# Centring the output projection's weights and the residual ahead of the layer norm of a hybrid decoder step

## The chip, the cores and the metric

One core of one Trainium2 chip. The metric is the device time of one execution in microseconds, the median of the runs shown; lower is better.

## The reference

One layer of a decoder over 1024 prompt tokens and 8 sample tokens (N = 1032 columns), d = 2048. The input projection feeds four head groups: A (gated DeltaNet), B (RWKV-7), C (forgetting attention, with a paged cache of 4096 positions for the samples) and D (causal pooling). Their gated outputs go through one output projection, and the result is normalised:

```python
gated = jnp.concatenate([o_A * _silu(z_A), o_B * _silu(z_B), o_C * _silu(z_C), o_D * _silu(z_D)], axis=-1)
out = jnp.einsum('nte,ed->ntd', gated, P['w_out'])
y = _layernorm(ALPHA_DN * x + out, P['ln_g'], P['ln_b'])
# _layernorm: mu = mean(x); var = mean((x - mu)^2); (x - mu) * rsqrt(var + 1e-5) * g + b
```

## The kernel before

Everything is held transposed, channels on partitions and tokens in columns. A float32 product is made of three fp32r matmuls (`mm3`, L306): weights and data are each split into a rounded half (`whi`, a cast on ACT, L302) and the rest (`wlo`, a subtraction on DVE, L303). Matmuls run on PE.

**Input projection.** 57 tiles of 128 output channels, each sixteen contraction tiles by three column groups of 344. Beside it run *fillers*: generators that `fill` (L316) advances four times a tile, each by its rate in yields per fill; what they issue between two yields stands at that place in program order. A scheduler then lays the instructions of each engine in one fixed order by its own estimate of their times, earlier program order first, so that an engine that is free runs ahead. Tiles 17 to 32 (`inputs`) are group A's; beside them run the preparation of A's operands (rate 1.6) and `start_b` (rate 1): the triangular inverses of B (`invert`, two pairs of heads) and the recurrent step of B for the samples (`sample_b`). In the 24 tiles that follow (`inputs_cd`, 96 fills) the inverses of A and the decode over the cached keys run at rate 1.6, the chains of B and A, the branch D and the first of branch C at rate 1. In `invert` the diagonal blocks go through a DRAM scratch (`UT`) and back into the tile `ivB` (L1176), one yield later 16 small matmuls read it (L1182), then a second set of small transfers fills `ivB` (L1190), and after one more yield the second set of matmuls follows (L1195). SP issues these transfers; it also issues the decay rows (`aogb`, `aobb`) and the stores of A's preparation.

**Attention** of branch C follows (`mixing`, about 1720 to 1920 us), with the decode over cached values (`decode_v`) as a filler that runs on into the third output pass.

**Output projection.** The contraction runs in four passes, one for each head group (`order`), because the groups are ready at different times. `self.y` (sixteen tiles of 128 x 1032) is the accumulator in SBUF. `out_pass` (L1700) does passes 0 to 2: for each tile `ct` 36 matmuls into three PSUM banks of tag `o` (five in all), then y += ps on DVE (L1720). In pass 2 it adds the residual first: y += ALPHA * x (L1714), x loaded on SP. Weights come as blocks of 128 x 512, fetched by `fetch` on ACT's queue into two `raw` buffers, split into two buffers each, and in the last pass into tiles that stay (`wkh`, `wkl`).

`out_last` (L1723) does pass 3 in three column groups of 392, 384 and 256, so that the normalisation of one group runs beside the matmuls of the next. PSUM starts with a matmul of a constant matrix of -16/2048 with the rounded y[0] (`mneg`, `yr`, L1765), which takes off a rough mean. Each tile is added to y (L1769), y is summed over tiles on DVE (L1775) and its square on ACT (L1776) and GpSimd, in the last group DVE (L1777). Then `norm` sums both over partitions with two matmuls (L1741), copies them (L1742), forms the variance, and per tile subtracts the mean (L1750), multiplies by the inverse root (L1751), both split between DVE and GpSimd by `NPOOL`, applies gain and bias on ACT (L1752) and stores on SP (L1753). `norm` is a filler of rate 1: its steps for a group stand between the tiles of the next.

Of the kernel before, what the change touches and what calls it, by code (L numbers as in the profile page):

```python
# [11 lines left out]
ALU = mybir.AluOpType  # L12
# [167 lines left out]
class Kernel:  # L180
# [94 lines left out]
    def weights(self, pool, srcs, pieces, keep=1 << 30):  # L275


        self.wp, self.wsrc, self.wraw, self.wsplit, self.wkeep, self.wn = pool, srcs, {}, {}, keep, pieces
# [855 lines left out]
    def invert(self, pool, br, pair, BD):  # L1134
# [42 lines left out]
        yield True  # L1177
# [13 lines left out]
        yield True  # L1191
# [494 lines left out]

    def gated(self, br, gp, stage):

        nc = self.nc
        gh = self.t(gp, [128, 4, N], "gh", F32R)  # L1690
        gl = self.t(gp, [128, 4, N], "gl", F32R)
        for i in range(4):
            r = self.t(stage, [128, N], "ostg")
            nc.sync.dma_start(r, self.G[4 * br + i])
            nc.scalar.copy(gh[:, i], r)  # L1695
            nc.vector.tensor_tensor(gl[:, i], r, gh[:, i].bitcast(F32), op=ALU.subtract)
        return gh, gl

    def out_pass(self, i, g, stage):
# [3 lines left out]
        for ct in range(16):  # L1703
# [19 lines left out]
    def out_last(self, i, g, stage, pool):  # L1723


# [10 lines left out]
        def norm(s, n, st):  # L1736
            s1, s2 = st
            sq = self.t(pool, [128, GROUPS[0]], "sq", bufs=2)[:, :n]
# [17 lines left out]
        for n in GROUPS:  # L1756
            s = slice(g0, g0 + n)
            st = [self.t(pool, [128, GROUPS[0]], x, bufs=2)[:, :n] for x in ("s1", "s2")]
            for ct in range(16):
# [5 lines left out]
                nc.tensor.matmul(ps, lhsT=mneg, rhs=yr[:, s], start=True, stop=False)  # L1765
                for j in range(4):
                    self.mm3(ps, hi[:, j], lo[:, j], gh[:, j, s], gl[:, j, s], False, j == 3)
                y = self.y[ct][:, s]
                nc.vector.tensor_tensor(y, y, ps, op=ALU.add)  # L1769
                if ct == 0:  # L1770
                    nc.vector.tensor_copy(st[0], y)
                    nc.scalar.activation(st[1], y, AF.Square)
                else:
                    sq = self.t(pool, [128, GROUPS[0]], "sq", bufs=2)[:, :n]
                    nc.vector.tensor_tensor(st[0], st[0], y, op=ALU.add)  # L1775
                    nc.scalar.activation(sq, y, AF.Square)  # L1776
                    (nc.gpsimd if ct <= SPOOL[GROUPS.index(n)] else nc.vector).tensor_tensor(st[1], st[1], sq, op=ALU.add)  # L1777
                self.fill()
            self.add(norm(s, n, st), 1)
# [4 lines left out]
    def build(self):  # L1784
# [10 lines left out]
        self.UT = tc.dram_tile([4, 16, 32, 32], F32, name="ut")  # L1795
        self.lfd = tc.dram_tile([8, 32, 1024], F32, name="lfd")
# [9 lines left out]
        with P(name="const", bufs=1) as cp, P(name="psum", bufs=2, space=PSUM) as self.psum0:  # L1806
# [18 lines left out]
            with P(name="psum2", bufs=2, space=PSUM) as self.psum1:  # L1825
                R = dict(side="right")
                with P(name="wo", bufs=2, **R) as wp, P(name="ost", bufs=2, **R) as sp, P(name="y", bufs=1, **R) as yp, \
# [3 lines left out]
                    self.weights(wp, [self.I["wo"][ct][:, 4 * br:4 * br + 4] for br in order for ct in range(16)], 1, 48)  # L1831
                    with P(name="g1", bufs=1) as g1:
# [13 lines left out]
                        self.out_pass(2, g[2], sp)  # L1846
                        self.drain()
# [6 lines left out]
    def inputs(self, cp, sp):  # L1854
# [19 lines left out]
        with P(name="aprep", bufs=1, **R) as ap:  # L1874
# [3 lines left out]
            self.add(self.start_b(), 1)  # L1878
# [14 lines left out]
    def start_b(self):  # L1893

        yield from self.inverses("B")
        with self.tc.tile_pool(reuse_waits="tile", name="smpB", bufs=1) as pool:
            yield from self.sample_b(pool)

# [68 lines left out]
```

## Time and profile before

| | us |
|---|---|
| runs shown | 2399.39, 2399.89 (median), 2400.68 |
| the profiled execution, its own time | 2396.94 |
| its span, first to last instruction | 2395.2 |
| busy: PE / PEld / DVE / ACT / GpSimd | 2282.6 / 2023.0 / 1364.7 / 938.4 / 295.0 |
| mean granted TensorE clock | 0.979 of full speed |

Matmuls are pipelined: the time from the start of one to the start of the next is what one costs, not its listed duration. PE is the matmul row, PEld its weight load, DVE is VectorE, ACT ScalarE, POOL GpSimd, SP the queue of SyncE. Idle time of an engine that is not the bottleneck costs nothing.

### The profile page before, as it was taken

The page shows a single profiled execution, that of the slowest core. Times are in us where ns is not written, and L with a number is a line of the kernel's source. Part 1 is how long each engine was busy: PE and PEld are TensorE (multiplying, and loading weights), DVE is VectorE, ACT ScalarE, POOL GpSimd, SP SyncE. Part 2 cuts the span into 40 slices and gives each one's busy share as a digit, 9 for nine tenths or more (in the row PEclk, how much of TensorE's full clock was granted, in tenths as well). Part 3 has the DMA queues.
Part 4 walks back from the last instruction along what each step waited for, and adds up shares of the span by engine and source line. Part 5 has one row for each costly group of instructions (what it writes and reads, how often), then busy time and mean ns, then how long its engine had stood idle before and what let it go on. Part 6 is the DMA issues. An engine that isn't in the chain of part 4 may idle for free. (4 is left out here: it accounts for less than half of the span.)

```text
span 2395.2 us, 47251 instructions
## 1 busy us (share of the span) xinstructions
PE 2282.6 (95%) x17640; PEld 2023.0 (84%) x17640; DVE 1364.7 (57%) x2676; ACT 938.4 (39%) x1853; POOL 295.0 (12%) x408
## 2 busy tenths in 40 slices
PE   8999999999899999999999999999899999999984
PEld 8999999998899999787787877899755578889984
DVE  4665757677576557432222245555578644564598
ACT  5644445434454444121111122454366665211244
POOL 0000000000000000103111121100132110100175
PEclk9999999999999999999999999999999999999997
DMA  6133323545523336778878888653488775683212
GB/s 215 56 100 95 104 85 95 151 106 120 113 81 94 89 107 142 172 187 264 274 250 283 259 273 288 232 161 107 124 260 248 223 282 192 219 304 129 88 63 88
DMA packets 369664, 402.44 MB, mean 168 GB/s; under 512 B 204877, under 2 KB 228350, under 8 KB 368666
## 3 DMA queue, kind: packets, MB, share of 16 engines
q1 hardware_dynamic: 307698, 263.83, 37.3%
q10 hardware_dynamic: 50056, 101.60, 13.9%
q0 software_dynamic: 11680, 33.99, 4.3%
q8 instruction: 139, 2.28, 0.4%
q14 instruction: 91, 0.75, 0.1%
HBM read 314.56 MB, written 84.67 MB: 167 GB/s over the span
## 5 line engine op out<-in xcount | busy, mean ns | idle before, releaser
L308 PE MATMUL pj<-xh,wlo 128*128 128x344 f32 x2688 | 873.1, 326 | 16.7 <-DVE wlo L303 8.6
L309 PE MATMUL pj<-xl,whi 128*128 128x344 f32 x2688 | 871.5, 324 | 0.0
L310 PE MATMUL pj<-xh,whi 128*128 128x344 f32 x2688 | 865.2, 324 | 0.0
L308 PEld LDWEIGHTS pj<-xh,wlo 128*128 128x128 f32 x2688 | 508.1, 189 | 37.1 <-issue 11.4
L309 PEld LDWEIGHTS pj<-xl,whi 128*128 128x128 f32 x2688 | 508.5, 189 | 19.8 <-issue 14.4
L310 PEld LDWEIGHTS pj<-xh,whi 128*128 128x128 f32 x2688 | 507.9, 189 | 16.4 <-issue 13.1
L302 ACT CAST whi<-raw 128x256 fp32r<-128x256 f32 (+1 forms) x504 | 213.0, 424 | 732.6 <-PE pj L310 530.2
L303 DVE TENSOR_TENSOR wlo<-raw,whi 128x256 fp32r<-128x256 f32 (+1 forms) x504 | 226.8, 452 | 365.5 <-ACT whi L302 356.1
L309 PE MATMUL o<-gl,whi 128*128 128x344 f32 x576 | 185.8, 323 | 0.0
L308 PE MATMUL o<-gh,wlo 128*128 128x344 f32 x576 | 184.6, 325 | 0.8 <-ACT gh L1695 0.5
L310 PE MATMUL o<-gh,whi 128*128 128x344 f32 x576 | 185.1, 321 | 0.0
L308 PEld LDWEIGHTS o<-gh,wlo 128*128 128x128 f32 x576 | 107.9, 188 | 21.8 <-DVE y L1720 9.4
L309 PEld LDWEIGHTS o<-gl,whi 128*128 128x128 f32 x576 | 109.0, 189 | 2.3 <-DVE ps L1221 0.9
L310 PEld LDWEIGHTS o<-gh,whi 128*128 128x128 f32 x576 | 109.0, 189 | 0.8 <-issue 0.8
L365 ACT ACTIVATE stg<-pj 128x344 f32<-128x344 f32 x168 | 74.6, 457 | 74.2 <-PE pj L310 73.0
L997 PE MATMUL k<-dkv,dqb 128*32 128x256 f32 x1024 | 88.4, 394 | 15.1 <-DMA dkv<-in_ck 9.0
L1720 DVE TENSOR_TENSOR y<-y,o 128x344 f32<-128x344 f32 x96 | 48.0, 510 | 57.3 <-PE o L310 57.0
L1105 PE MATMUL k<-dkv,dpT 128*8 128x512 f32 x512 | 71.5, 635 | 0.8 <-DMA dkv<-in_cv 0.8
L861 DVE TENSOR_TENSOR cpl<-cpt,cph 128x512 fp32r<-128x512 f32 (+1 forms) x96 | 60.9, 653 | 15.7 <-ACT cph L860 14.9
L308 PE MATMUL o<-gh,wkl 128*128 128x392 f32 (+2 forms) x192 | 63.9, 333 | 0.6 <-DVE wkl L303 0.5
L310 PE MATMUL o<-gh,wkh 128*128 128x392 f32 (+2 forms) x192 | 63.6, 331 | 0.0
L309 PE MATMUL o<-gl,wkh 128*128 128x392 f32 (+2 forms) x192 | 63.3, 330 | 0.0
(597 smaller groups left out, 3321.9 us busy)
## 6 DMA issues: line engine op xcount, KB each, us to landing
dkv<-in_ck SPq DMA_DIRECT2D x256, 256.0 KB
dkv<-in_cv SPq DMA_DIRECT2D x256, 256.0 KB
raw<-in_w ACTq DMA_DIRECT2D x228, 256.0 KB
out_pj<-stg ACTq DMA_DIRECT2D x33, 516.0 KB
bop<-bop SPq DMA_DIRECT2D x16, 1024.0 KB
raw<-in_wo ACTq DMA_DIRECT2D x64, 256.0 KB
aop<-aop SPq DMA_DIRECT2D x16, 768.0 KB
aop<-aost SPq DMA_DIRECT2D x40, 256.0 KB
```

Of the source, the lines that this page charges most:

```text
L302: nc.scalar.copy(hi, raw)
L303: nc.vector.tensor_tensor(lo, raw, hi.bitcast(F32), op=ALU.subtract)
L308: nc.tensor.matmul(ps, lhsT=wlo, rhs=xh, start=start, stop=False)
L309: nc.tensor.matmul(ps, lhsT=whi, rhs=xl, start=False, stop=False)
L310: self.last = nc.tensor.matmul(ps, lhsT=whi, rhs=xh, start=False, stop=stop).ins
L365: self.nc.scalar.activation(dst[:, g * G3:g * G3 + G3], ps[g], func)
L861: nc.vector.tensor_tensor(pl[:, off:], pt[:, off:], ph[:, off:].bitcast(F32), op=ALU.subtract)
L997: nc.tensor.matmul(ps[32 * hp:32 * hp + 32], lhsT=qb[:, hp, b], rhs=kt[:, :, hp], start=b == 0, stop=b == 7)
L1105: mm = lambda i: nc.tensor.matmul(po[32 * i:32 * i + 8], lhsT=pTv[:, c, :, 4 * bg + i], rhs=t[i // 2][:, i % 2], start=False, stop=c == 31)
L1720: nc.vector.tensor_tensor(y[:, s], y[:, s], ps[g], op=ALU.add)
```

## The change

The mean over channels is taken out before the normalisation instead of in it. `centre`, a new end of `start_b` (whose rate goes from 1 to 1.45), reads the whole output matrix once more, 64 blocks of 256 KB on SP with up to five in flight, and sums each row's blocks on DVE; the negative row mean `wm` stays in SBUF. It also reads x in 32 halves on GpSimd's queue, adds them there, and by two matmuls a column group gets ALPHA times the mean of x, which goes to DRAM (`XM`). The splits of the output weights subtract the mean (four activations and four DVE operations a block in place of one and one). In pass 2 the mean is loaded again and GpSimd subtracts it from each y tile, three tiles at the first step and then one a step, two ahead. What remains of y has zero mean over channels, so `out_last` loses the `mneg` matmul, the running sum of y, its column sum, the variance correction and the subtraction. In `invert` two of the waits of one yield become three, for B and for A.

```diff
             raw = self.wraw[j][:, w * (n % p):w * (n % p) + w]
-            nc.scalar.copy(hi, raw)
-            nc.vector.tensor_tensor(lo, raw, hi.bitcast(F32), op=ALU.subtract)
+            if self.wless:
+                m = self.wless(n)
+                for k in range(4):
+                    nc.scalar.activation(hi[:, k], raw[:, k], AF.Identity, bias=m[:, k:k + 1])
+                    nc.vector.scalar_tensor_tensor(lo[:, k], raw[:, k], m[:, k:k + 1], hi[:, k].bitcast(F32),
+                                                   op0=ALU.add, op1=ALU.subtract)
...
@@ invert, after the load of BD from UT, and after the second set of loads
-        yield True
+        for _ in range(3):
+            yield True
...
+    def centre(self, keep):
+        self.wm = self.t(keep, [128, 16], "wm")
+        with self.tc.tile_pool(reuse_waits="tile", name="cen", bufs=1) as pool:
+            part = self.t(pool, [128, 16, 16], "wpart")
+            xs = self.t(pool, [128, N], "csum")
+            R, H = [], N // 2
+            def load():
+                ct, br = divmod(len(R), 4)
+                R.append(self.t(pool, [128, 4, 128], "cw", bufs=5))
+                nc.sync.dma_start(R[-1], self.I["wo"][ct][:, 4 * br:4 * br + 4])
+            for n in range(64):
+                while len(R) < min(n + 5, 64):
+                    load()
+                if n % 2 == 0:
+                    yield 1
+                ct, br = divmod(n, 4)
+                nc.vector.reduce_sum(part[:, 4 * br:4 * br + 4, ct], R[n], axis=AX.X)
+                if n < 32:
+                    k, s = n // 2, slice(H * (n % 2), H * (n % 2) + H)
+                    x = xs[:, s] if k == 0 else self.t(pool, [128, H], "cx", bufs=2)
+                    nc.gpsimd.dma_start(x, self.I["xT"][k, :, s])
+                    if k:
+                        nc.gpsimd.tensor_tensor(xs[:, s], xs[:, s], x, op=ALU.add)
+            nc.vector.reduce_sum(self.wm, part, axis=AX.X)
+            nc.vector.tensor_scalar(self.wm, self.wm, -1.0 / D, None, op0=ALU.mult)
...
+            for g in range(3):
...
+                yield 1
+                ps = self.ps("b", (128, G3))
+                nc.tensor.matmul(ps, lhsT=m2k, rhs=lo, start=True, stop=False)
+                nc.tensor.matmul(ps, lhsT=m2k, rhs=hi, start=False, stop=True)
+                nc.scalar.activation(xs[:, s], ps, AF.Copy, scale=ALPHA)
+            nc.sync.dma_start(self.XM, xs)
...
@@ out_pass
             if i == 2:
+                for c in range(0 if ct == 0 else ct + 2, min(ct + 3, 16)):
+                    nc.gpsimd.tensor_tensor(self.y[c], self.y[c], self.xm, op=ALU.subtract)
                 xr = self.t(stage, [128, N], "ostg")
...
@@ out_last
-        mneg = self.t(pool, [128, 128], "mneg", F32R)
-        nc.vector.tensor_scalar(mneg, m2k, -16.0, None, op0=ALU.mult)
-        yr = self.t(stage, [128, N], "ostg", F32R)
-        nc.scalar.copy(yr, self.y[0])
...
-            for x in (s1, s2):
-                ps = self.ps("b", (128, n))
-                nc.tensor.matmul(ps, lhsT=m2k, rhs=x, start=True, stop=True)
-                nc.vector.tensor_copy(x, ps)
-            nc.scalar.activation(sq, s1, AF.Square)
-            nc.vector.tensor_tensor(s2, s2, sq, op=ALU.subtract)
-            self.rsqrt(s2, s2, self.eps["ln"])
+            ps = self.ps("b", (128, n))
+            nc.tensor.matmul(ps, lhsT=m2k, rhs=s2, start=True, stop=True)
+            self.rsqrt(s2, ps, self.eps["ln"])
...
-                e.tensor_tensor(y, y, s1, op=ALU.subtract)
                 e.tensor_tensor(y, y, s2, op=ALU.mult)
...
-                nc.tensor.matmul(ps, lhsT=mneg, rhs=yr[:, s], start=True, stop=False)
...
-                    nc.vector.tensor_tensor(st[0], st[0], y, op=ALU.add)
...
@@ build, around pass 2
+                        with P(name="xm", bufs=1) as pp:
+                            self.xm = self.t(pp, [128, N], "xm")
+                            nc.sync.dma_start(self.xm, self.XM)
+                            self.out_pass(2, g[2], sp)
+                            self.drain()
@@ inputs
-            self.add(self.start_b(), 1)
+            self.add(self.start_b(cp), 1.45)
```

## Rows read from the trace of the kernel before

**Rows 1.** The page's first part: engine, busy us (share of the span), instructions.

```profile
PE 2282.6 (95%) x17640; PEld 2023.0 (84%) x17640; DVE 1364.7 (57%) x2676; ACT 938.4 (39%) x1853; POOL 295.0 (12%) x408
```

**Rows 2.** Busy time by stage: length, busy us (count) by engine, clock, DMA.

```profile
760.00:895.00 135.00, 135.00 (x1119) 131.51 (x1118) 76.44 (x133) 63.34 (x125) 0.76 (x3) 1.00 0.35 98
...
970.00:1090.00 120.00, 108.88 (x1210) 95.00 (x1211) 45.86 (x121) 22.37 (x51) 18.22 (x29) 0.97 0.72 182
...
2288.00:2395.20 107.20, 68.72 (x411) 64.63 (x409) 95.79 (x139) 47.58 (x89) 71.79 (x62) 0.82 0.22 80
```

**Rows 3.** Waits from 2250 us on: who, us in total, times, longest.

```profile
PE o L1765 <- DVE y L1769: 14.7, 6, 5.3
```

**Rows 4.** Groups on DVE, 2280 to 2395: count, busy us, mean ns, idle.

```profile
L1750 DVE TENSOR_TENSOR y<-y,s 128x392 f32<-128x392 f32 (+2 forms) x25 | 25.5, 1081 | 0.1
...
L1775 DVE TENSOR_TENSOR s<-s,y 128x384 f32<-128x384 f32 (+2 forms) x36 | 24.0, 665 | 0.6
...
L1769 DVE TENSOR_TENSOR y<-y,o 128x384 f32<-128x384 f32 (+2 forms) x37 | 17.8, 487 | 2.2 <-PE o L310 2.2
```

**Rows 5.** Timeline of PE, last pass: start us, us, instruction, idle before.

```profile
2246.23 0.44 PE L1765 MATMUL o<-ostg,mneg 128*128 128x392 f32 x1 [1.42 <-DVE mneg L1731]
...
2292.96 0.34 PE L1765 MATMUL o<-ostg,mneg 128*128 128x384 f32 x1
...
2295.24 0.34 PE L1765 MATMUL o<-ostg,mneg 128*128 128x384 f32 x1
...
2331.77 0.28 PE L1765 MATMUL o<-ostg,mneg 128*128 128x256 f32 x1
...
2333.30 0.28 PE L1765 MATMUL o<-ostg,mneg 128*128 128x256 f32 x1
...
2367.78 0.28 PE L1765 MATMUL o<-ostg,mneg 128*128 128x256 f32 x1
```

**Rows 6.** Timeline of ACT, the last group's Ln.

```profile
2381.84 0.51 ACT L1234 ACTIVATE s<-s,epsln 128x256 f32<-128x256 f32 x1 [4.06 <-DVE s L1744]
```

**Rows 7.** Weights: first fetch and last split (timeline); groups of ACT by shape.

```profile
2246.08 1.06 ACTq L292 DMA_DIRECT2D raw<-in_wo  x2
...
2280.69 0.69 DVE L303 TENSOR_TENSOR wkl<-raw,wkh 128x512 fp32r<-128x512 f32 x1 [0.34 <-ACT wkh L302]
...
L302 ACT CAST wkh<-raw 128x512 fp32r<-128x512 f32 x16 | 9.9, 619 | 28.3 <-DMA raw<-in_wo 27.1 <-DVE wlo L303 1.1
...
L1223 ACT ACTIVATE asq<-asq,epsone 128x512 f32<-128x512 f32 x24 | 17.3, 721 | 0.7 <-DVE ivU L1165 0.4
```

**Rows 8.** Timeline of DVE and POOL about 2290 us: alone, then side by side.

```profile
2290.16 0.56 DVE L1775 TENSOR_TENSOR s<-s,y 128x384 f32<-128x384 f32 x1
...
2291.23 11.09 DVE L1750 TENSOR_TENSOR y<-y,s 128x392 f32<-128x392 f32 x9
...
2291.27 9.32 POOL L1750 TENSOR_TENSOR y<-y,s 128x392 f32<-128x392 f32 x7 [2.20 <-DVE s L1742]
```

**Rows 9.** Waits of PE, 900 to 1100 us.

```profile
PE k L1182 <- DMA ivB<-ut: 6.9, 2, 4.6
```

**Rows 10.** Groups of DVE by shape: a reduction of 512 columns.

```profile
L789 DVE TENSOR_REDUCE cmx<-b 128x1 f32<-128x512 f32 x24 | 16.4, 686 | 3.8 <-PE b L785 3.5
```

**Rows 11.** Groups of POOL by shape.

```profile
L911 POOL TENSOR_TENSOR cnum<-cnum,cden 128x1024 f32<-128x1024 f32 x4 | 9.5, 2386 | 30.8 <-ACT cden L908 30.8
...
L1777 POOL TENSOR_TENSOR s<-s,sq 128x392 f32<-128x392 f32 x15 | 15.8, 1051 | 66.4 <-ACT sq L1776 66.4
```

**Rows 12.** DMA issues: count, KB each, median us to landing.

```profile
pz<-out_pj POOLq DMA_DIRECT2D x8, 256.0 KB, 5.2
```

**Rows 13.** Stores of sample states: B (tile view), A (POOL's timeline).

```profile
L1483 POOL DMA_DIRECT2D out_oBS<-sS x1: 552/552/552, 760.6 to 760.6; - x1
...
2131.25 0.55 POOL L1483 DMA_DIRECT2D out_oAS<-sS  x1 [39.66 <-DVE sS L1481]
```

**Rows 14.** Waits of PE, 620 to 780 us.

```profile
PE pj L308 <- ACT stg L365: 5.6, 1, 5.6
```

More of the change, by code (lines that the diff above doesn't have):

```diff
@@ L273, in load_x, with weights @@
             nc.vector.tensor_tensor(self.xl[k], r, self.xh[k].bitcast(F32), op=ALU.subtract)
-    def weights(self, pool, srcs, pieces, keep=1 << 30):
+    def weights(self, pool, srcs, pieces, keep=1 << 30, less=None):
+        self.wless = less
         self.wp, self.wsrc, self.wraw, self.wsplit, self.wkeep, self.wn = pool, srcs, {}, {}, keep, pieces
@@ L301, in fetch @@
                 raw = self.wraw[j][:, w * (n % p):w * (n % p) + w]
-                nc.scalar.copy(hi, raw)
-                nc.vector.tensor_tensor(lo, raw, hi.bitcast(F32), op=ALU.subtract)
+                if self.wless:
[4 more added lines that the diff above has]
+                                                       op0=ALU.add, op1=ALU.subtract)
+                else:
+                    nc.scalar.copy(hi, raw)
+                    nc.vector.tensor_tensor(lo, raw, hi.bitcast(F32), op=ALU.subtract)
                 self.wsplit[n] = hi, lo
@@ L1190, in invert @@
                 nc.sync.dma_start(BD[b, q::4, b], OP[m::4, p1, hp, off + 32:off + 64].rearrange("c p i -> p c i"))
-        yield True
+        for _ in range(3):
+            yield True
         ps = self.ps("k")
@@ L1684, in sample_b @@
         yield from self.state_step(pool, S, w, [(k, v), (a, sn)], O["oBS"], "B")
+    def centre(self, keep):
+        nc = self.nc
+        self.wm = self.t(keep, [128, 16], "wm")
[22 more added lines that the diff above has]
+            nc.vector.tensor_scalar(self.wm, self.wm, -1.0 / D, None, op0=ALU.mult)
+            m2k = self.t(pool, [128, 4, 128], "cw", F32R, bufs=5)[:, 0]
+            nc.vector.tensor_scalar(m2k, self.onec.to_broadcast([128, 128]), 1.0 / D, None, op0=ALU.mult)
+            P = []
+            for g in range(3):
+                s = slice(g * G3, g * G3 + G3)
+                hi, lo = (self.t(pool, [128, 4, 128], "cw", F32R, bufs=5).rearrange("p k m -> p (k m)")[:, 0:G3] for _ in range(2))
+                nc.scalar.copy(hi, xs[:, s])
+                nc.vector.tensor_tensor(lo, xs[:, s], hi.bitcast(F32), op=ALU.subtract)
+                yield 1
[4 more added lines that the diff above has]
+            nc.sync.dma_start(self.XM, xs)
     def gated(self, br, gp, stage):
@@ L1757, in out_last @@
             s = slice(g0, g0 + n)
-            st = [self.t(pool, [128, GROUPS[0]], x, bufs=2)[:, :n] for x in ("s1", "s2")]
+            s2 = self.t(pool, [128, GROUPS[0]], "s2", bufs=2)[:, :n]
             for ct in range(16):
@@ L1764, in out_last @@
                 ps = self.ps("o", (128, n))
[L1765 removed]
                 for j in range(4):
[L1767 removed]
+                    self.mm3(ps, hi[:, j], lo[:, j], gh[:, j, s], gl[:, j, s], j == 0, j == 3)
                 y = self.y[ct][:, s]
@@ L1770, in out_last @@
                 if ct == 0:
-                    nc.vector.tensor_copy(st[0], y)
-                    nc.scalar.activation(st[1], y, AF.Square)
+                    nc.scalar.activation(s2, y, AF.Square)
                 else:
                     sq = self.t(pool, [128, GROUPS[0]], "sq", bufs=2)[:, :n]
-                    nc.vector.tensor_tensor(st[0], st[0], y, op=ALU.add)
                     nc.scalar.activation(sq, y, AF.Square)
-                    (nc.gpsimd if ct <= SPOOL[GROUPS.index(n)] else nc.vector).tensor_tensor(st[1], st[1], sq, op=ALU.add)
+                    (nc.gpsimd if ct <= SPOOL[GROUPS.index(n)] else nc.vector).tensor_tensor(s2, s2, sq, op=ALU.add)
                 self.fill()
-            self.add(norm(s, n, st), 1)
+            self.add(norm(s, n, s2), 1)
             g0 += n
@@ L1795, in build @@
         self.UT = tc.dram_tile([4, 16, 32, 32], F32, name="ut")
+        self.XM = tc.dram_tile([128, N], F32, name="xm")
         self.lfd = tc.dram_tile([8, 32, 1024], F32, name="lfd")
@@ L1830, in build @@
                     order = (3, 1, 0, 2)
-                    self.weights(wp, [self.I["wo"][ct][:, 4 * br:4 * br + 4] for br in order for ct in range(16)], 1, 48)
+                    self.weights(wp, [self.I["wo"][ct][:, 4 * br:4 * br + 4] for br in order for ct in range(16)], 1, 48,
+                                 lambda n: self.wm[:, 4 * order[n // 16]:4 * order[n // 16] + 4])
                     with P(name="g1", bufs=1) as g1:
@@ L1891, in inputs_cd, with start_b @@
         self.drain()
-    def start_b(self):
+    def start_b(self, keep):
         yield from self.inverses("B")
@@ L1897, in start_b @@
             yield from self.sample_b(pool)
+        yield from self.centre(keep)
     def cached(self):
```

6 lines of the change are left out of this document (1 added, 5 removed).

## Prediction

> **What bounds the kernel now.** I read the page's first part, then a table by stage, then the waits, groups and timeline of the last stage. The page says matmul: PE is busy 95% of the span [rows 1]. By stage this holds until about 2288 us, while from 2288 to the end PE is busy 68.7 of 107.2 us and DVE 95.8 [rows 2]. That stage is DVE's. PE stands there 14.7 us in the last pass's centring matmul until DVE has emptied a PSUM bank by y += ps [rows 3]: in DVE's queue the normalisation of the group before is ahead of it. In 2280 to 2395 DVE spends 25.5 us on y -= mean and 24.0 us on the running sum of y [rows 4]; the change deletes both. The pass starts at 2246.23, group 2 paces at 2.28 us a column tile (2295.24 less 2292.96), group 3 runs from 2331.77 at 1.53 (2333.30 less 2331.77), and its last tile starts at 2367.78 [rows 5], where sixteen tiles at 1.53 need only 24.5 us of the 37. From the last Ln (2381.84) to the end of the span, 2395.2, are 13.4 us [rows 6].
>
> **The last pass after the change**, in four steps, against this run (span 2395.2, time 2396.94; the median of the runs shown is 2399.89, 2.95 above it, so I put the difference on the median).
> (a) Start: PE no longer waits 1.42 us for the -1/128 matrix [rows 5]. -1.4.
> (b) Group 1 fetches its weights by two staging buffers: from the issue at 2246.08 to the fourteenth split at 2280.69 + 0.69 are 35.3 us, 2.52 a block [rows 7], above PE's need (twelve matmuls of 392 columns at 0.175 x 392/384, 2.15). So the deleted matmul is hidden here. The split becomes 4 + 4 instructions. A cast of 512 columns is 0.619; an activation with a bias pointer is 0.721 on 512 columns, 0.10 more [rows 7]. Bounds for one of 128: a quarter of the second, 0.18, and the whole cast, 0.62. I take 0.32 (the fixed part overlaps the previous one), so 1.3 a block, +0.65 on ACT; DVE's last quarter follows it by about 0.35 instead of 0.69. A buffer's turn grows by 0.3 and 14 blocks at 2.67 take 37.4, 2 us more. PE then ends behind the last block: 2244.9 + 37.4 + 2.15, about 2284.5, where before group 2 started near 2287. -1; bounds -5 (PE alone) and +8 (0.62 each).
> The Trainium skill (ScalarE: Activation LUTs, What ACT_TABLE_LOAD costs) gives 280 ns + 0.833 ns a column with a bias pointer, 93 ns overlapped; by it a block's four would be an estimated 1.27 us. The rows of 512 agree (0.721 against 0.707); no row has 128 columns.
> (c) Group 2: twelve matmuls at 0.175 by sixteen, 33.7, plus 0.7 for a column sum, against 44.8 (about 2287 to 2331.77). -10.4. DVE keeps sixteen adds of 0.49 [rows 4] and nine multiplications of 0.56 to 1.23 (11.09/9 with GpSimd active, 0.56 alone [rows 8]), 19 us at most; GpSimd has fifteen square sums and seven products of 1.05 alone [rows 11] to 1.33 (9.32/7 [rows 8]), 23 to 29: both fit beside PE. Group 3: 16 x 12 x 0.118 = 22.6 plus 0.7 against 37.5 (2331.77 to 2367.78 + 1.5). -14.2. DVE has there 16 adds and 15 square sums, up to 0.49 each, and seven products of 1.23 at most, 24 at the worst for 23: barely covered, and late next.
> (d) Tail: from the last tile's start (2367.78) plus 1.5 to 2381.84 were 12.6 us. What stays is an add, a square, a sum (up to 0.49 each [rows 4]), one column matmul of some 0.7 and perhaps 1.5 of backlog: 3.6. -9. The last 13.4 us stay; ACT's sixteen affine steps set them.
> Together -36; I take **-33** for stalls that remain, bounds -22 and -40.
>
> **Inverses.** Two waits of one yield become three, so the block matmuls stand later in PE's order than the small transfers that they need. PE waited 6.9 us for them in the A inverse [rows 9], and it is idle 11 of 120 us from 970 to 1090 [rows 2]. The eight added yields at rate 1.6 delay the A inverse by 5 of the phase's 96 fills; it had 2 to spare before the first use of a query tile (fill 16), its 65 later steps end near fill 60, and the keys come at 64 anyway: nothing late next. I take **-8**, bounds 0 and -13.
>
> **The centring work (start_b).** 30 + 22 + 35 yields at rate 1.45 are 60 of 64 fills: it ends inside the phase. DVE gets 64 reductions of 512 columns at 0.686 [rows 10], 44 us, from about 718 to 895: sample B's last store came at 760.6 [rows 13] after 44 fills of about 6 us, and will come after 52/1.45 = 36, near 712, plus the landing. There DVE is busy 76.4 of 135 us [rows 2], so 43% of 177 us, 76, is free. GpSimd gets 30 adds; by 1.05 for 392 columns and 2.386 for 1024 [rows 11] one of 516 is 1.32, 40 us. Nine DVE ops took 11.09 us beside seven GpSimd ops instead of 9 x 0.56 = 5.0 [rows 8], 6 us lost in 9.3 of GpSimd. If DVE loses two thirds of 40, it needs 71 of 76: covered, just.
> The skill (SBUF — State Buffer, Who interferes with whom) calls it an exclusive lock which a reduction never takes; by it the 44 us could run inside GpSimd's 40. Rows 8 show the lock's cost for two SBUF inputs; no run here has a reduction beside GpSimd. The sum stays on the bounds above.
> POOL's x loads: 256 KB land in 5.2 us [rows 12], two buffers, so (about 0.55 to issue + 5.2 + 1.32)/2 = 3.5 us a half, 32 of them 113 us, ending near 830, before the closing matmuls (fill 58, near 845). SP gets 64 loads of 256 KB, each waiting for a reduction, and behind them on SP stand the decay rows (aogb) and the stores of the A preparation. Six PE matmuls cost 2 us. Stalls: bounds 0 and 40 (the slow rival); I take **+8** in all.
>
> **Passes 1 to 3.** Splits: +0.65 ACT and about +0.5 DVE on 48 blocks. A split starts when PE frees the buffer and PE then has a whole block, 5.7 us (36 x 0.157), in hand: hidden; 0 to +8, I take +1. Subtractions: 16 x 2.4 [rows 11] = 38 us of POOL in a pass of 91 us. They take the load of the mean with them: its room was sample A's state, whose store is issued at 2131.25 [rows 13]; with some 8 us to land (1 MB; 256 KB take 5.2 [rows 12]) and 5 to load, the first y -= xm ends near 2147 and the first x-add near 2149, when the pass's first block is done (estimate). Five banks are 1 2/3 blocks of grace. Bounds 0 and +12; I take +1. On SP the cache pages stand behind that load, four tiles ahead of use.
>
> Sum: -33 - 8 + 8 + 1 + 1 = **-31**, so 2396.9 becomes 2366 and the median 2399.9 becomes **2369**.
>
> **Rivals.**
> 1. *Given back at the end* (chance 0.20, about 2385). GpSimd carries square sums and products in groups 2 and 3, and its op grows from 1.05 [rows 11] to 1.33 beside DVE [rows 8]; if its chain sets the column sums and ACT's sixteen steps wait, half the 33 stays. For: today's late sums. Against: the subtractions, half of GpSimd's share of the normalisation, are gone.
> 2. *The centring stalls the A phase* (0.13, about 2410, slower). Place: SP's queue from 718 to 895. Once before, near 640, ACT stood behind a late decay row, PSUM was not emptied and PE lost 5.6 us [rows 14]. There are four such rows in the stretch; with loads waiting for reductions ahead of them, and weights late where DVE falls behind, 4 x 5.6, some 2 each at the low clock after a stall, and 20 of late splits make 50. It decides from 39 up: then -33 - 8 + 2 is used up. Against: PE lost nothing there with DVE at 57% [rows 2], and the splits have priority.
> 3. *The third pass waits for the mean* (0.10, about 2384): the mean's load late or subtractions behind another GpSimd wait, PE idle for 15 or so. Against: 2.4 a block against 5.7.
> 4. *No net change* (0.04): the deleted DVE work was slack. Against: rows 3.
> The forecast itself has 0.53.
>
> **Numbers.** About 0.2% (5 us) is what a measurement of this kernel can tell from no change. Forecast, 1 and 3 are faster but for scraps: 0.80. Same: 0.06. Slower, rival 2 with a scrap of 1 and 3: 0.14. The range runs from -40 at the end and -10 elsewhere (2350) to just past no change (2403), leaving rival 2's body outside. Faster cases alone: 2350 to 2390.
>
> **What would show it.** Right: in the last stage PE waits for y += ps under 4 us, DVE's busy time from 2288 on falls by 50 or more, the stage from the pass's first matmul to the end takes 113 to 120 us instead of 149; PE's idle from 970 to 1090 under 5; PE over 97% busy while the reductions run. Wrong: the pass still ends on DVE or GpSimd sums; waits of PE for weight splits or ACT's evacuation between 700 and 900 of more than 15 us; PE idle at the start of pass three.

## The result, and the profile after

The changed kernel takes 2424.63 us (median of 4 executions, 2419.39 to 2427.70) beside 2399.64 for the kernel before on the same chip: a ratio of 1.0102, 95% interval 1.0078 to 1.0126, about 25 us slower. I had forecast 2369, with a range of 2350 to 2403. Of the profiled execution (2425.16 us, span 2423.3), the page's first part, to be read beside [rows 1]:

```profile
PE 2290.6 (95%) x17592; PEld 2028.2 (84%) x17592; DVE 1415.3 (58%) x2855; ACT 982.0 (41%) x2047; POOL 369.0 (15%) x463
```

PE does 48 matmuls fewer, and the span is 28 us longer: PE waits elsewhere. Busy time by stage (columns as in [rows 2]), while the sums run, in the A inverse, while the third pass's subtractions run, and for the last 107.2 us:

```profile
764.00:868.00 104.00, 94.81 (x690) 92.38 (x689) 93.76 (x142) 37.62 (x75) 50.53 (x54) 0.93 0.92 289
970.00:1090.00 120.00, 109.08 (x1198) 98.41 (x1197) 53.65 (x143) 26.44 (x56) 11.24 (x17) 0.96 0.74 177
2176.00:2217.00 41.00, 26.95 (x131) 22.56 (x130) 38.85 (x21) 3.84 (x12) 40.78 (x16) 0.76 0.40 132
...
2316.10:2423.30 107.20, 84.23 (x510) 79.98 (x510) 66.23 (x122) 64.18 (x136) 54.75 (x50) 0.92 0.29 100
```

The last stretch is most of what was hoped for: DVE 66.2 busy where [rows 2] has 95.8, PE 84.2 where it has 68.7. The A inverse is as it was. The first and the third row are new: DVE full and PE waiting, at the start of the third pass with a granted clock of 0.76. The third pass as a whole, from its first weight matmul to that of the last pass, before and then after:

```profile
2147.90:2246.50 98.60, 97.18 (x621) 90.51 (x620) 47.46 (x82) 15.02 (x21) 0.75 (x1) 1.00 0.37 123
2185.90:2301.60 115.70, 100.42 (x597) 91.21 (x589) 87.61 (x135) 24.53 (x68) 35.00 (x14) 0.91 0.43 144
```

Every run is read by one table, from each kernel's timeline, in us. "To 28" is the time at which ACT begins to split the weights of projection tile 28 (counted from 0), "28-35" from there to tile 35 (in it the sums), "35-end" to the end of the last projection matmul, "mixing" to the first output matmul, "pass 0" to its last PSUM evacuation, "pass 1-2" to the first matmul with weights of the last pass, "last" to the end of the span.

```
kernel               to 28  28-35  35-end  mixing  pass 0  pass 1-2   last    span   ratio to before
before               751.9  178.8   786.9   202.9   114.8   211.3    148.7  2395.2
after                752.9  202.2   786.7   217.7   110.5   231.5    121.7  2423.3  1.0102
e1_sub_dve           756.4  204.2   788.3   214.7   111.2   215.1    119.9  2409.8  1.0031
e8_no_centre         752.7  179.8   781.1   202.4   115.2   214.8    120.3  2366.3  0.9892
e16_no_centre_rate1  738.6  180.7   796.8   198.1   117.8   215.0    120.2  2367.2  0.9866
e2_no_xsum           757.3  210.8   785.4   202.4   116.8   231.1    121.5  2425.3  1.0100
e3_no_reduce         751.0  188.7   790.4   210.1   117.9   231.8    122.4  2412.3  1.0057
e5_resident          756.7  209.0   799.2   195.3   118.4   232.0    120.4  2431.0  1.0151
e11_act_loads        747.2  210.5   794.6   203.1   115.2   213.7    121.2  2405.5  1.0043
e15_one_buf          753.5  227.6   806.1   225.2   114.3   214.3    120.1  2461.1  1.0262
e6_dma_sums          745.9  256.0   789.5   199.7   117.6   214.4    120.2  2443.5  1.0218
e7_dma_all           754.6  255.5   788.6   204.2   116.5   241.5    119.6  2480.5  1.0306
e9_after_inverse     741.2  181.7   804.0   221.6   117.3   214.8    122.9  2403.7  1.0036
e12_rate22           739.8  182.1   834.3   221.2   113.5   214.2    122.4  2427.6  1.0119
e13_rate30           739.0  184.3   836.4   222.8   111.9   215.2    121.5  2431.1  1.0094
e14_late             741.6  181.3   814.0   230.4   113.9   216.0    121.5  2418.7  1.0075
e4_inverse           741.0  182.5   786.2   200.7   116.9   211.2    148.8  2387.4  0.9961
e17_inverse_145      756.0  179.8   789.5   201.4   114.7   211.2    148.9  2401.5  1.0002
```

In the changed kernel the last stage gives 27 us; 28-35 takes 23, passes 1 and 2 take 20, and mixing takes 15. The subtraction in the third pass is on GpSimd in e2, e3 and e5, as in the changed kernel; in e7 a DMA does it, and in the other runs with the changed last pass it is on DVE.

### The profile page after: what moved, and what is told of

The parts are those of the page before. It is cut to its first block, busy times and chain, and to the rows that moved or that the text cites. A ratio compares the mean times of both kernels' runs of the same rounds, so it can differ in the third digit from the quotient of the medians.

```text
span 2423.3 us, 47768 instructions
## 1 busy us (share of the span) xinstructions
PE 2290.6 (95%) x17592; PEld 2028.2 (84%) x17592; DVE 1415.3 (58%) x2855; ACT 982.0 (41%) x2047; POOL 369.0 (15%) x463
## 5 line engine op out<-in xcount | busy, mean ns | idle before, releaser
L316 PEld LDWEIGHTS pj<-xh,wlo 128*128 128x128 f32 x2688 | 509.2, 190 | 43.5 <-issue 15.3
L317 PEld LDWEIGHTS pj<-xl,whi 128*128 128x128 f32 x2688 | 510.0, 190 | 18.3 <-issue 13.7
L310 ACT CAST whi<-raw 128x256 fp32r<-128x256 f32 x456 | 183.3, 404 | 581.4 <-PE pj L318 523.3
L311 DVE TENSOR_TENSOR wlo<-raw,whi 128x256 fp32r<-128x256 f32 x456 | 200.3, 441 | 313.7 <-ACT whi L310 303.9
L306 ACT ACTIVATE whi<-raw,wm 128x128 fp32r<-128x128 f32 x192 | 61.4, 391 | 154.3 <-PE o L318 81.1
L307 DVE SCALAR_TENSOR_TENSOR wlo<-raw,wm,whi 128x128 fp32r<-128x128 f32 x192 | 74.4, 436 | 16.4 <-ACT whi L306 16.2
## 6 DMA issues: line engine op xcount, KB each, us to landing
dkv<-in_ck SPq DMA_DIRECT2D x256, 256.0 KB
dkv<-in_cv SPq DMA_DIRECT2D x256, 256.0 KB
raw<-in_w ACTq DMA_DIRECT2D x228, 256.0 KB
cw<-in_wo SPq DMA_DIRECT2D x64, 256.0 KB
raw<-in_wo ACTq DMA_DIRECT2D x64, 256.0 KB
```

Source lines behind the costliest of these rows:

```text
L306: nc.scalar.activation(hi[:, k], raw[:, k], AF.Identity, bias=m[:, k:k + 1])
L307: nc.vector.scalar_tensor_tensor(lo[:, k], raw[:, k], m[:, k:k + 1], hi[:, k].bitcast(F32), op0=ALU.add, op1=ALU.subtract)
L316: nc.tensor.matmul(ps, lhsT=wlo, rhs=xh, start=start, stop=False)
L317: nc.tensor.matmul(ps, lhsT=whi, rhs=xl, start=False, stop=False)
```

## Experiments: the subtraction in the third pass

**e1_sub_dve.** `- nc.gpsimd.tensor_tensor(self.y[c], ..., self.xm, ...)` / `+ nc.vector.tensor_tensor(...)`

> The sixteen subtractions of the x mean in the third output pass run on VectorE (about 1.2 us each, in order with its other work) instead of on GpSimd; all else as in the changed kernel. Passes 1 and 2 together (from the second pass's first matmul to the last pass's first matmul) took 209 us before and 230 us after. Theory (GpSimd's back-to-back subtractions of 2.4 us hold off every two-SBUF-operand operation of VectorE, the weight splits first): passes 1 and 2 take 205 to 215, TensorE waits for weight splits fall from 14 us to under 4, the total is 2403 to 2412. Rival (the 4 + 4 small split instructions or the late load of the mean cost the time, wherever the subtraction runs): passes 1 and 2 stay at 225 or more, and VectorE's added 20 us make the total 2425 or more.

Measured: 2407.01 us, ratio 1.0031 (1.0008 to 1.0054); passes 1 and 2 215.1, at the edge of the 205 to 215 expected. The theory holds. PE's wait in the third pass, after:

```profile
PE o L316 <- DVE wlo L307: 14.3, 8, 4.4
```

It is absent in e1. The timeline of POOL and DVE, after, shows why (start us, us, instruction, count; idle before):

```profile
2176.22 24.33 POOL L1767 TENSOR_TENSOR y<-y,xm 128x1032 f32<-128x1032 f32 x9 [13.99 <-DMA xm<-xm]
...
2182.45 3.02 DVE L1770 SCALAR_TENSOR_TENSOR y<-ostg,y 128x1032 f32<-128x1032 f32 x1
2185.40 0.50 DVE L1776 TENSOR_TENSOR y<-y,o 128x344 f32<-128x344 f32 x1
2185.82 6.80 DVE L307 SCALAR_TENSOR_TENSOR wlo<-raw,wm,whi 128x128 fp32r<-128x128 f32 x3
```

And the two groups of e1 in its third pass:

```profile
L307 DVE SCALAR_TENSOR_TENSOR wlo<-raw,wm,whi 128x128 fp32r<-128x128 f32 x60 | 17.5, 346 | 0.0
L1770 DVE SCALAR_TENSOR_TENSOR y<-ostg,y 128x1032 f32<-128x1032 f32 x14 | 17.1, 1230 | 4.0 <-DMA ostg<-in_xT 4.0
```

GpSimd runs its subtractions back to back, 2.70 each (24.33/9). A DVE instruction with two SBUF inputs needs 1.23 undisturbed and takes 3.02 beside them; a weight piece needs 0.35 and takes 2.27 (6.80/3). The add from PSUM stays at 0.50. So each two-input DVE instruction is 1.8 to 1.9 longer, whatever its size, about two thirds of a GpSimd instruction, and four small pieces in place of one split pay that four times (no run has the undivided split there).

## Experiments: the sums in the A preparation

**e8_no_centre**: the generator `centre` becomes two memsets and the store of XM; subtraction on DVE.

> The sums are left out altogether (weight mean and x mean are zero), the subtraction in the third pass stays, on VectorE, and the fillers keep the rate of 1.45 (yT isn't centred). Theory (the sums are the whole loss in the A preparation): tile 28 to tile 35 takes 175 to 183 us, mixing 200 to 212, passes 1 and 2 213 to 217, last stage 120 to 122, total 2362 to 2378. Rival (the higher rate of the fillers by itself puts the preparation late): tile 28 to 35 takes 190 or more, total 2380 or more.

Measured: 2370.37 us, ratio 0.9892 (0.9865 to 0.9919). 28-35 is back at 179.8, mixing at 202.4. Against e1, whose only difference is the sums, 1.4% (1.0031 less 0.9892), some 33 us, is their price. The two profiled executions differ by more, 43.5: 24 in 28-35, 12 in mixing, 7 in 35-end. The stretch of the sums in this kernel:

```profile
764.00:868.00 104.00, 104.00 (x853) 101.62 (x852) 60.43 (x105) 50.32 (x99) 0.20 (x2) 1.00 0.33 88
```

DVE has 60.4 us of work here without any sums. With 43 of reductions that would be 103 of 104; the 93.8 seen above are less because part of the preparation's work was pushed out behind (142 instructions, 64 of them reductions, where this kernel has 105).

**e2_no_xsum**: `- if n < 32:` / `+ if n < 2:`

> The 30 additions of x on GpSimd and their loads are left out of the centring (its x mean is that of one tile, so yT is changed by a shift that the norm's mean no longer removes exactly); the 64 weight reductions on VectorE stay. By the time tile 35 of the projections was emptied the changed kernel had lost 22 us since tile 28. Theory (the additions hold off VectorE's two-operand work, on which the A preparation's matmuls wait): that loss falls under 8, total 2405 to 2413. Rival (the 64 reductions, run ahead in VectorE's queue in about 100 us, make the preparation late by themselves): the loss stays at 15 or more, total 2418 or more.

**e3_no_reduce**: the loads and `reduce_sum` of the weight blocks out, `+ nc.vector.memset(self.wm, 0.0)`.

> The 64 loads and reductions of the output weights are left out (the subtracted weight mean is zero, so yT isn't centred); the x additions on GpSimd stay. Theory (both together fill VectorE: 44 us of reductions and some 40 us held off by GpSimd): the loss between tiles 28 and 35 is under 10, of the 22. If the additions alone did it: 15 or more. If the reductions alone did it: under 4. Mixing (end of projections to the first output pass, 203 us before, 218 after): theory, an order of instructions that depends on where the fillers stood; it may come out between 200 and 220 here.

**e5_resident**: `- while len(R) < min(n + 5, 64):` / `+ while len(R) < 5:`, and `R[n]` becomes `R[n % 5]`.

> As the run without the x additions, but only the first five weight blocks are loaded and the 64 reductions read those five over and over, so DVE has the same 44 us of reductions and no loads stand behind them (the weight means are wrong, yT isn't centred). From the split of tile 28 to that of tile 35 the kernel before took 179 us, the run without additions 211. Theory (VectorE's queue stands on reductions whose block hasn't landed, 18 us in that run, and weight loads are late beside them): falls to 190 or less, total 2392 to 2406. Rival (44 us of reductions in the way of the A preparation's chain are enough): stays at 200 or more, total 2412 or more. If it is under 184 although the reductions run, the amount of VectorE work does nothing.

Measured: e2 2421.72 us (1.0100; 1.0066 to 1.0134), 28-35 210.8; e3 2414.21 (1.0057; 1.0032 to 1.0083), 188.7; e5 2434.14 (1.0151; 1.0119 to 1.0183), 209.0. My theory fell in e2 and in e5. Without the additions the loss is no smaller (32 us), so neither the additions nor DVE's waiting beside them is its main cause; the additions alone cost 10. And with no loads behind them the reductions cost as much (30), so the loads aren't needed for it either. DVE's timeline after, where the sums begin:

```profile
767.39 0.69 DVE L1717 TENSOR_REDUCE wpart<-cw 128x4 f32<-128x512 f32 x1
767.99 0.74 DVE L425 SCALAR_TENSOR_TENSOR am<-stg,par,am 128x512 f32<-128x512 f32 x1
770.32 0.69 DVE L1717 TENSOR_REDUCE wpart<-cw 128x4 f32<-128x512 f32 x1 [1.59 <-DMA cw<-in_wo]
770.92 1.51 DVE L311 TENSOR_TENSOR wlo<-raw,whi 128x256 fp32r<-128x256 f32 x1
772.35 0.68 DVE L1231 SCALAR_TENSOR_TENSOR asq<-am 128x512 f32<-128x512 f32 x1
...
773.29 1.27 DVE L1717 TENSOR_REDUCE wpart<-cw 128x4 f32<-128x512 f32 x2
774.54 1.58 DVE L1234 SCALAR_TENSOR_TENSOR asq<-am,asq 128x512 f32<-128x512 f32 x1
776.04 2.00 DVE L311 TENSOR_TENSOR wlo<-raw,whi 128x256 fp32r<-128x256 f32 x1
777.96 0.67 DVE L1717 TENSOR_REDUCE wpart<-cw 128x4 f32<-128x512 f32 x1
778.56 0.68 DVE L1239 TENSOR_TENSOR am<-am,asq 128x512 f32<-128x512 f32 x1
```

and in e5:

```profile
771.07 0.74 DVE L425 SCALAR_TENSOR_TENSOR am<-stg,par,am 128x512 f32<-128x512 f32 x1
771.73 7.21 DVE L1717 TENSOR_REDUCE wpart<-cw 128x4 f32<-128x512 f32 x12
```

am, asq, am again is one chain of the A preparation, and ACT and PE have steps between its links. DVE's queue is in a fixed order, and one or two reductions stand before nearly every link; in e5 twelve stand in one row, and 24 before the next link of am. The work that follows the chain is late, and idle time behind does not bring it back: in e5 DVE has idle time again from 800 on (us and columns as above), and the 30 stay lost.

```profile
760.00:800.00 40.00, 36.62 (x216) 36.34 (x215) 33.35 (x60) 8.02 (x19) 1.09 (x2) 0.91 0.32 105
800.00:840.00 40.00, 34.87 (x235) 33.72 (x235) 27.59 (x54) 15.64 (x31) 0.10 (x1) 0.91 0.24 64
840.00:880.00 40.00, 39.49 (x344) 38.06 (x345) 22.10 (x39) 20.56 (x39) 0.10 (x1) 1.00 0.30 83
```

PE waits at the end of the chain (after, PE's waits from 760 to 940; [rows 2] show none in such a stretch):

```profile
PE a L471 <- DVE am L462: 6.3, 2, 3.5
PE pj L316 <- ACT stg L373: 3.5, 1, 3.5
PE b L1547 <- DVE hsl L1546: 2.9, 1, 2.9
PE a L471 <- DVE aoeg L466: 2.0, 1, 2.0
```

**e11_act_loads**: `- nc.sync.dma_start(R[-1], ...)` / `+ nc.scalar.dma_start(R[-1], ...)`; the subtraction on DVE, as in e1.

> The weight blocks to be summed are asked for on ScalarE's queue, in order with the PSUM evacuations, instead of on SyncE's; all else as in the run with the subtraction on VectorE (2407; tile 28 to 35 204 us). The order on VectorE is the same, with one or two reductions in front of most steps. Theory (the order on VectorE sets the loss): stays at 195 to 210, total 2400 to 2412. Rival (the loads run ahead and press reductions and other transfers into the first 100 us; paced by ScalarE they spread): 190 or less, total 2395 or less. If ScalarE stands on full buffers: over 215.

Measured: 2409.66 us (1.0043; 1.0023 to 1.0064), 28-35 210.5: against e1 (1.0031, 204.2) nothing is gained, so which engine's queue asks for the blocks is not what costs.

**e15_one_buf**: `cw` with one buffer instead of five, so that one block at a time is asked for, in its own step; the subtraction on DVE.

> Sums in the A preparation as in the run with the subtraction on VectorE (2407; tile 28 to 35 204 us), but the weight blocks have one buffer in place of five, so each load waits for the reduction before it, and the 64 reductions are spread over 265 of VectorE's instructions instead of 139. Theory (it is the density of the reductions in VectorE's queue, ahead of the A preparation's chain): tile 28 to 35 takes 182 to 195 us, total 2385 to 2400. Rival (the same 44 us cost the same loss however they are spread, or VectorE stands on the single buffer's loads): 200 or more, total 2405 or more.

Measured: 2462.89 us (1.0262; 1.0236 to 1.0288), 28-35 227.6. Spread out like this, the sums cost more, but the run does not test density alone: DVE now stands on the blocks. Its largest wait, 760 to 945 us:

```profile
DVE wpart L1717 <- DMA cw<-in_wo: 55.3, 33, 4.2
```

A reduction whose block hasn't landed holds everything behind it. So there are two prices, which the runs show apart: the reductions' own time ahead of the chain (e5, no loads) and DVE standing on a late load (here; in e2 the same wait is 17.8 us). Whether reductions spread thinly, with their blocks at hand, would be free, no run shows.

**e6_dma_sums** and **e7_dma_all**: the sums by accumulating DMAs, the subtraction on DVE; in e7 a DMA does the third pass's subtraction too.

```
+            for ct in range(16):
+                op = dict(accum_op=ALU.add) if ct else {}
+                for h in range(2):
+                    nc.gpsimd.dma_start(acc[h], self.I["wo"][ct][:, 8 * h:8 * h + 8], **op)
+                nc.gpsimd.dma_start(xs, self.I["xT"][ct], **op)
...
+                nc.gpsimd.dma_start(xr, self.XM, accum_op=ALU.add)
```

> Both sums are made by accumulating DMAs: 16 x 2 loads of half a weight tile added into two accumulators in SBUF, 16 loads of x added into a third, issued by GpSimd; VectorE is left with two reductions of 1024 columns in place of 64 of 512, GpSimd with no addition. The subtraction in the third pass is on VectorE. Theory: the preparation is hardly disturbed, tile 28 to tile 35 takes 178 to 187 us; total 2365 to 2385, faster than the kernel before. Rival (25 MB of extra transfers in that stretch make the weights late, whoever adds): 195 or more, total 2388 or more.

> As the run with accumulating sums, and the subtraction in the third pass goes too: the negative mean is added to each x tile by an accumulating DMA behind its load, so no engine has it. Passes 1 and 2 took 210 us before, 231 after, 215 with the subtraction on VectorE. Theory: 208 to 212 here, total 2360 to 2380. Rival (the accumulation comes late and y = x * alpha + y waits for it): 214 or more and waits of VectorE for x tiles.

Measured: e6 2448.00 us (1.0218; 1.0187 to 1.0249), 28-35 256.0; e7 2470.70 (1.0306; 1.0280 to 1.0333), passes 1 and 2 241.5. Both rivals hold. In e6 764 to 868:

```profile
764.00:868.00 104.00, 70.90 (x536) 68.92 (x535) 31.65 (x56) 26.64 (x54) 27.38 (x34) 0.82 1.00 209
```

DVE is nearly empty (31.7), and PE waits more than ever: the DMA engines are full (share 1.00) at 209 GB/s, where the changed kernel's plain loads moved 289 at 0.92. ACT then waits for the preparation's own stores (e6, 760 to 945), and in e7 DVE for the accumulated x (2242 to 2361):

```profile
ACT aost L474 <- DMA aop<-aost: 33.0, 3, 20.0
```

```profile
DVE y L1757 <- DMA ostg<-xm: 40.5, 9, 9.5
```

## Experiments: the sums elsewhere

**e9_after_inverse**: `yield from self.centre(...)` from the end of `start_b` to behind the A inverse in `cached`; rate 1.45 back to 1; the subtraction on DVE, as in all four. **e12_rate22**, **e13_rate30**: the same with RATE_L 2.2 and 3.0 in place of 1.6. **e14_late**: x summed from the resident tiles behind the A inverse, the weights behind the cache keys with two buffers.

> Both sums as in the changed kernel, but their place is behind the A inverse, among the recurrent work of the next stage, where VectorE is busy 24 to 49 per cent of a stretch instead of 57 and the A preparation is over; the fillers of the preparation go back to rate 1, the subtraction is on VectorE. Theory (a reduction in front of each step of the A preparation's chain is what costs; where no such chain feeds TensorE the same 44 us are nearly free): tile 28 to 35 takes 176 to 183 us, from there to the end of the projections at most 10 more than the 787 before, total 2362 to 2385, faster than the kernel before. Rival (44 us of VectorE and 25 MB of loads cost 20 us wherever they are, since the loads compete with the cache loads at a DMA share of 0.85 there): projections end 20 later than in the run without sums, total 2385 or more.

> The sums stay behind the A inverse, as in the run before (2408), and the rate of that chain of fillers goes from 1.6 to 2.2, so that the cache keys, which the 35 added pauses put off by 123 to 165 us (last key matmul at 1644 instead of 1521), come about where they were. Theory (that run lost its gain because the keys and what hangs on them came after the projections' cover had gone): last key matmul before 1570, end of projections 1705 to 1718, total 2365 to 2385, faster than the kernel before. Rival (the added loads and reductions cost their 20 us wherever they stand): projections end at 1725 or later, total 2395 or more.

> The same with a rate of 3.0. Theory: keys earlier still, last key matmul before 1500; total within 10 us of the run with 2.2. Rival (fillers too dense: the A inverse's steps run into their transfers and TensorE waits): waits for the inverse's blocks over 15 us where they are 8, total 2395 or more. The mixing stage has taken 195 to 222 us in the runs so far, in no order that I can read from the place of the sums.

> The sums leave the A preparation: x is summed by GpSimd from the rounded x that lies in SBUF (15 additions of 1032 columns, no loads) behind the A inverse, and the weight blocks are loaded and summed behind the cache keys, from about 1520 us on, where the DMA share of before falls from 0.82 to 0.58 and 0.33 and no preparation's chain stands in VectorE's queue; two buffers. Subtraction on VectorE, preparation fillers at rate 1. Theory (what costs is the place: VectorE's chain in one stage, the key loads' DMA time in the next): tile 28 to 35 176 to 183, keys end before 1560, projections end 1706 to 1722, total 2362 to 2385, faster than before. Rival (44 us of reductions cost some 20 us wherever they stand): projections end at 1728 or later or mixing takes over 215, total 2390 or more.

Measured: e9 2407.90 us (1.0036; 1.0016 to 1.0056), e12 2427.92 (1.0119; 1.0087 to 1.0151), e13 2419.75 (1.0094; 1.0062 to 1.0125), e14 2417.23 (1.0075; 1.0051 to 1.0100). In all four 28-35 is free of loss, and the price comes back later. In e9 the key matmuls (weight loads; count, ns, first to last start) stand 165 and 123 us later than in e8:

```profile
L1005 PEld LDWEIGHTS k<-dkv,dqb x1024: 106/109/110, 1252.3 to 1644.2; 128*32 128x32 f32 x171
```

and in e8:

```profile
L1005 PEld LDWEIGHTS k<-dkv,dqb x1024: 106/109/154, 1087.7 to 1520.9; 128*32 128x32 f32 x171
```

Against e4, which has the same rate and no sums, e9 loses 18 us in 35-end and 21 in mixing: the projections run ahead of the keys and no longer cover them. A higher filler rate does not bring the keys forward (1248.9 to 1645.3 in e12), so my reading that the rate put them off is wrong. The keys stand behind the sums in one chain of fillers; that its 25 MB of loads pace it, I read from the DMA share of 0.92 to 0.97 from 1100 to 1200 us in e9, and no run shows it alone. In e14 DVE stands on the blocks again (1480 to 1740):

```profile
DVE wpart L1738 <- DMA cw<-in_wo: 33.0, 25, 4.3
```

The theory of the place falls too: no place that I tried was free. Against e16 below (0.9866), which has the rate of 1 and no sums, e9's sums cost some 41 us, no less than in the preparation. Spreading the sums over several stages, a branch at a time, was not tried.

## Experiments: the inverses

**e4_inverse**: the kernel before with only this, at both places: `- yield True` / `+ for _ in range(3): yield True`. **e17_inverse_145**: e4 with `start_b` at 1.45. **e16_no_centre_rate1**: e8 with it at 1.

> The kernel before with only the two longer pauses in the inverses (three yields in place of one at two places). Theory: TensorE's waits for the block transfers shorten, but the stretch of the A inverse gains little: total 2392 to 2400, mixing stage about 203 us. Rival (the moved fillers put the mixing stage's work in a worse order): mixing takes 212 or more and the total is 2403 or more. My forecast had -8 for it: 2391.

> The kernel before with the longer pauses in the inverses (2388) and the fillers of the preparation at 1.45. Theory: the gain is gone, tile 28 at 746 to 757, total 2394 to 2402. Rival: tile 28 at 738 to 743 and 2385 to 2391.

> As the run without any sums (2370; weight mean and x mean are zero, yT isn't centred), with the preparation's fillers at rate 1 instead of 1.45. In five kernels at rate 1 with the longer pauses tile 28 was split at 739 to 742 us, in nine at 1.45 at 746 to 757. Theory (the longer pauses gain their 8 to 10 us in the B inverse, and the raised rate that the sums need gives it back): tile 28 at 738 to 743, total 2358 to 2366. Rival (what differs between those kernels is something else, the place of the sums): tile 28 at 748 or later, total 2368 or more.

Measured: e4 2387.96 us (0.9961; 0.9937 to 0.9984): my -8 is there, and this version is faster than both kernels. e17 2400.17 (1.0002; 0.9979 to 1.0024): gone. e16 2367.25 (0.9866; 0.9835 to 0.9898): tile 28 at 738.6 instead of 752.7, but 35-end is 15.7 longer, and the total is the same as e8's within the two intervals. So e4's gain is made before tile 28, beside the B inverse, and in e17 the rate of 1.45 takes it back; that the lower rate would give it back to the changed kernel is not shown. PE's waits from 560 to 760 us in e4, where the kernel before had the 5.6 of [rows 14]:

```profile
PE k L1197 <- DMA ivB<-bop: 3.6, 1, 3.6
PE k L1183 <- DMA ivB<-ut: 1.0, 1, 1.0
```

and in the changed kernel that wait stands as it was:

```profile
PE pj L316 <- ACT stg L373: 5.6, 1, 5.6
```

The wait that the pauses were meant to shorten is as long in e4 (945 to 1130) as the 6.9 of [rows 9]:

```profile
PE k L1183 <- DMA ivB<-ut: 6.9, 2, 5.2
```

## Why the prediction was wrong

**The last pass** (-33 forecast; -27.0 measured, 120 to 123 us in all kernels that have it, against 148.7): right in mechanism, at the small side of its bounds. Group 1 took 38.7 (2301.58 to 2340.29; 1.6 of its matmuls come later) where steps (a) and (b) gave 39.6; a split piece on ACT costs what (b) took for it, four in 1.28. Group 2 took 38.0 instead of 34.4, and group 3 28.2 (to 2406.5) instead of 23.3, so step (c) is the one that was mis-sized. DVE has time enough beside PE (busy 19.9 of the 28.2 in group 3), but its work comes in the wrong order: from 2385 on it does seven multiplications in a row, 8.28 us, ahead of the adds that empty PSUM; PE stands 3.1 and then runs 2395 to 2400 at a granted clock of 0.66. Step (d) held: from there to the last Ln 3.1, and 13.7 behind it. PE's, DVE's and ACT's rows after:

```profile
2301.58 0.45 PE L316 MATMUL o<-gh,wkl 128*128 128x392 f32 x1 [0.89 <-DVE wkl L307]
...
2340.29 0.34 PE L316 MATMUL o<-gh,wkl 128*128 128x384 f32 x1
...
2378.33 0.28 PE L316 MATMUL o<-gh,wkl 128*128 128x256 f32 x1
```

```profile
PE o L316 <- DVE y L1812: 4.8, 2, 3.1
```

```profile
2180.09 1.28 ACT L306 ACTIVATE whi<-raw,wm 128x128 fp32r<-128x128 f32 x4 [5.58 <-DMA raw<-in_wo]
```

```profile
2385.17 8.28 DVE L1795 TENSOR_TENSOR y<-y,s 128x384 f32<-128x384 f32 x7
```

```profile
L1795 DVE TENSOR_TENSOR y<-y,s 128x392 f32<-128x392 f32 (+2 forms) x25 | 26.2, 1116 | 2.1 <-ACT s L1245 2.0
```

The 14.7 of [rows 3] became 4.8. A multiplication by the inverse deviation still costs 1.12 on DVE beside GpSimd's, as the subtraction of [rows 4] did (1.08).

**The centring work** (+8 forecast, some +33 measured: e8 against e1). The step that failed is "43% of 177 us, 76, is free ... it needs 71 of 76: covered, just". It treated DVE's idle time as room for any work. The reductions did not spread over the 177 us; they ran from 764 to 868, 104 us in which DVE has 44 free without them (60.4 busy in e8) and they alone took 43. The start was forecast for 718, since the raised rate was to bring the last store of sample B's state from 760.6 to near 712; it was issued at 755.7, and the loads wait for it:

```profile
L1493 POOL DMA_DIRECT2D out_oBS<-sS x1: 557/557/557, 755.7 to 755.7; - x1
```

```profile
SPq L1710 <- DMA out_oBS<-sS: 16.4, 1, 16.4
```

And the idle time lies between the links of the preparation's chain: a reduction put before a link moves the link. How much of the 24 us in 28-35 is the full queue and how much the order in it, no run separates. My bound of +40 held the value. What I had rested the sum on, DVE losing two thirds of GpSimd's 40 us, was the smaller part (e3: 10). The rival that came out was the second, in its stage and near its price, but not by the decay rows that it named: ACT's largest waits in the changed kernel's stretch are for PE and DVE. Its time, 2410, is not the one measured; 2424.63 is what rivals 2 and 3 make together (3 adds 15), and the forecast had priced each by itself.

**The subtractions** (+1 forecast, 0 to +12; about +17 measured against the same work on DVE, 1.0102 against 1.0031). The step that failed is "2.4 a block against 5.7": it spread sixteen instructions over sixteen blocks, and counted GpSimd's time alone. They ran together, all sixteen begun between 2176.2 and 2216.7, and [rows 8] already showed what DVE pays beside them (11.09 us for nine instructions of 0.56). That the mean comes late, rival 3, is in the row as well (13.99 us of idle POOL before the first), but it delayed little: e1 loads the same mean and loses 4.

The Trainium skill (SBUF — State Buffer, Who interferes with whom) has one exclusive lock between DVE and GpSimd, held for a whole instruction. The trace agrees: 0.35 became 2.27 beside instructions of 2.70, and the reductions stayed at 0.67 to 0.69 in the midst of the additions. I had cited it, and had not put its price on the split pieces.

**The inverses** (-8): right in number alone (e4, some -9), and that by luck. The waits for the block transfers, which the pauses were to shorten, did not shrink (6.9 in e4, and the changed kernel still idles 10.9 us of 970 to 1090); what went is the 5.6 of [rows 14], a wait for ACT. Which of the moved transfers did that stays open. And the raised rate, which I had costed at nothing, takes the gain away (e17).

**Mixing** was in no step. It took 198 to 203 us in the five kernels without sums and 195 to 230 in those with them. So it is the sums that scatter it, but not by their presence alone (e5 has the shortest); which order of instructions makes it long I leave open.

The parts measured, -27, +33, +17 and nothing for the inverses, make +23 of the 25 us; mixing's share is inside the 33.

## What to carry to other kernels

Idle time of an engine that serves a chain is not free room: work put into its in-order queue delays the links that it stands before, and more when its own load is late. Count the free time in the stretch where the work will really run, and ask what decides when it starts. Before moving sums to a quiet engine, ask which instructions of its neighbour take two SBUF operands, and count most of one foreign instruction for each of them (here 1.8 to 1.9 of 2.70); splitting one instruction into four multiplies that price by four. And time each part of a change alone: of the four parts here one gained 9 us by itself, one 27 in its own stage, and the other two cost 33 and 17.

## What the runs showed of the hardware that was not expected

In the stretch with the accumulating DMAs (e6) the DMA engines were full (share 1.00) at 209 GB/s, where with plain loads of the same data (the changed kernel) they reached 289 at 0.92; other transfers run in both. A load of 512 KB into the accumulators landed after 8.2 us (median of 32, thirty of them accumulating), plain ones of 512 KB on the same queue after 6.4 to 7.2. GpSimd's subtraction of 1032 columns took 2.70 beside a busy DVE against 2.39 for 1024 in [rows 11]. An add with one operand in PSUM was untouched, 0.50 beside it and without it.
